# Pads that set where matmul operands lie, mod 512 bytes, in a two-block transformer kernel

## The chip, the core and the metric

The kernel runs on one core of a Trainium2 chip, as one program and one launch. The metric is the device time of a run in microseconds. The kernel before was timed in three runs: 1470.07, 1471.21 and 1471.54 us, median 1471.21 us.

## The reference

One sequence of 256 tokens with 1024 features goes through two layers of a first block and one layer of a second block, all in float32.

A layer of the first block computes

```
proj   = x @ w_in                       # queries, keys, values, gMLP halves, gates
out_a  = window_attention(...)          # 8 heads over 2 key heads, with a sink
out_b  = dense_block_attention(...)     # 8 heads over 2 key heads
out_c  = spatial_gating(u, v, ...)      # gMLP
merged = (branches @ w_branch * sigmoid(gate + b_gate)).sum over the branches
x = layer_norm(ALPHA * x + merged @ w_mix_out)
x = layer_norm(ALPHA * x + cross_attention(x, mem) @ x_wo)
x = layer_norm(ALPHA * x + gated_conv_ffn(x) @ f_w_down)   # 1024 -> 2 x 2816 -> 1024
```

The second block normalises x, takes one large product with w_in, runs a gated linear recurrence over 1344 channels and a sparse attention of 16 heads, merges both through gates, and adds an MLP of width 4096:

```
merged = sigmoid(g_a) * (y_a @ proj_a) + sigmoid(g_b) * (y_b @ proj_b)
h = x + merged @ w_out
out = h + square(relu(rmsnorm(h) @ w_mlp_in)) @ w_mlp_out
```

Nearly all of the arithmetic is the weight products.

## The kernel before

**Weights.** Class `Stream` brings the weights from HBM in the order of their use, in chunks of 128 partitions by 1024 float32 (512 KB), into four rotating tiles `raw`. Each chunk is split: ScalarE writes a rounded float32r part `wh` (L220), VectorE the rest `wl` (L221). There are four tiles of each, and two chunks are split ahead of the one in use.

**Products.** Activations are kept in two float32r parts too, so a product is three matmuls: high by high, low by high, high by low. There are two forms.

- `mm_a` (L402 to L404) gives a feature-major result. A 128x128 piece of the weight chunk is the stationary operand, and 256 tokens of activations (128x256) are the moving one. A chunk holds eight pieces, so it gives 24 matmuls.
- `mm_b` (L416 to L418, and L427, L455 to L458 for first chunks) gives a token-major result. A 128x128 piece of activations is stationary, and 512 columns of the weight chunk (128x512) are moving.

Each matmul is preceded by its own load of the stationary operand, which TensorE's queue starts while the matmul before is still streaming.

**The activations' tiles.** `fm` (`fmh`, `fml`) holds the features of the running x, or a merged result, for `mm_a` (gates, u, up, min and so on) and for `mm_b` (qa, v, mix, wq ...). `o` (`oh`, `ol`) holds a branch's output, moving in the `br` products (L402 to L404) and stationary in `wo`. `mem` holds the memory; `a` (`ah`, `al`) the FFN's hidden layer, stationary in `down`; `ya` the recurrence's output, moving in `pa`; `mg` the second block's merged result, stationary in `wo2`; `z` (`zh`, `zl`) the last MLP's hidden layer, stationary in `mout`.

**Order.** TensorE's instructions stand in the order in which the program is written, with attention units put in between at fixed ticks (`tick`, L341); the other engines' are ordered by the scheduler, in favour of what was written first. Nothing in the change touches these. Around a sublayer's end (`finish`, L570) the last chunks of a product and the first of the next are placed in other free room (`w0` to `w3`, `k4`, `a` and `fm` tiles).

**Places.** Tiles are laid out in SBUF by stacked pools: `base`, `w` (`raw`, `wh`, `wl`), `fm`, `sm`, then pools that are opened and closed by sublayer. A tile's place is the sum of the sizes before it, and since most sizes are multiples of 512 bytes a partition, all weight tiles `wh` and `wl` of the stream lie at 128 mod 512, and so do all `fm` tiles.

Of the kernel before, what the change touches and what calls it, by code (L numbers as in the profile page):

```python
# [47 lines left out]
def pack_a(w, nw=128, kw=128, per=8):  # L48
    """[K, N] -> one chunk of `per` stationary tiles after the other, N outer and K inner."""
    k, n = w.shape  # L50
    t = w.reshape(k // kw, kw, n // nw, nw).transpose(2, 0, 1, 3).reshape(-1, kw, nw)
    c = t.shape[0] // per
    return np.ascontiguousarray(t.reshape(c, per, kw, nw).transpose(0, 2, 1, 3).reshape(c, kw, per * nw))


def pack_b(w):
    """[K, N] -> chunks of two 128-row tiles of 512 columns, N outer and K inner."""
    k, n = w.shape
    t = w.reshape(k // 128, 128, n // 512, 512).transpose(2, 0, 1, 3).reshape(-1, 2, 128, 512)
    return np.ascontiguousarray(t.transpose(0, 2, 1, 3).reshape(-1, 128, 1024))  # L60


def feat(v, w=128):
    """[..., N] -> [w, ..., N // w]: features on partitions."""
# [11 lines left out]
def layout(x):  # L76
    """The arrays the program reads: the inputs cut and ordered, and constants of the shapes."""
# [96 lines left out]
class Stream:  # L174
    """The weights in the order of their use: each chunk comes in ahead of its products and is split
    into two float32r parts whose sum is the float32 weight."""
# [10 lines left out]
    def load(self, i, piece=None):  # L187
# [7 lines left out]
        else:  # L195
            # the very first chunk, in two pieces of 512 columns
# [46 lines left out]
    def take_last(self, key, places, more):  # L243
        """The last chunks of a product, as many as places and two, and those behind them, all on chip at once;
        those behind the first two have their room in places, the third one behind and on in more."""
# [5 lines left out]
    def hold(self, after):  # L251
        """The next chunks are split after the instructions `after`."""
# [3 lines left out]
class Program:  # L256
    def __init__(self, ctx, tc, a, out):
# [41 lines left out]
        # products that raise the tensor engine's clock while the first loads are on their way  # L299
# [21 lines left out]
    # ---- small helpers  # L321
# [18 lines left out]
    # ---- the order of the tensor engine: a tick before the products of each chunk  # L340
    def tick(self):  # L341
        """Gives out what is due, then a step of everything in the background."""
# [14 lines left out]
    def spawn(self, g):  # L357
        """Runs the first step of g now, the others a tick apart."""
# [3 lines left out]
    def wait(self):  # L362
        """What follows on the vector engine comes after the split of the last chunk."""
        return self.tc.issue_after(self.w.last.ins)

    def settle(self):
        """Gives out all that is left in the background."""
# [3 lines left out]
    def rstd(self, pool, var, eps, n, scale=1.0):  # L371
        """(var * scale + eps) ** -0.5 in float32, Newton's method from the exponent halved."""
# [13 lines left out]
    def split(self, h, l, src):  # L386
        """float32r parts h + l of src (SBUF or PSUM)."""
# [7 lines left out]
    def mm_a(self, ps, w, xs, nw=128, kw=128, t0=0, start=True, stop=True):  # L395
        """ps [nw, S] += W^T x: stationary tiles t0.. of the chunk w against the feature-major xs."""
# [9 lines left out]
    def mm_b(self, outs, ws, xs, kt, ts=(0, 1)):  # L406
        """outs[t] [128, 512] += x W for chunk list ws covering k-tiles kt.. of kt_n."""
# [12 lines left out]
    def mm_b_first(self, outs, wt, xs):  # L420
        """mm_b with the very first chunk, in the order in which the parts come."""
# [8 lines left out]
    def proj_b(self, key, xs, kn=8):  # L430
        """Token-major product with a [K, 512] weight."""
# [9 lines left out]
    def proj_first(self, key, xs):  # L441
        """Token-major product with a [1024, 512] weight, one token tile after the other; yields, each time with
        the outputs, before the passes of a token tile with the low parts of xs[:4] and xs[4:], and at the end."""
# [17 lines left out]
    def proj_second(self, key, xs, n):  # L461
        """Token-major product with a [1024, 512] weight: its first n chunks with the first token tile, then,
        after a yield, the rest; yields the outputs at the end."""
# [9 lines left out]
    def turn(self, outs, n, done):  # L473
        """Feature-major tiles [128, 2, S] of a token-major product: done(i, tile) n ticks later."""
# [15 lines left out]
    def take_early(self, key):  # L490
        """Takes the chunks that come before the next one of `key`."""
# [3 lines left out]
    def proj_last(self, key, xs, kn, places, more, done):  # L495
        """Token-major product with a [K, 1024] weight, the first token tile done some chunks ahead of the
        second. done(t, half, out) follows as soon as an output is whole; yields after each token tile."""
# [23 lines left out]
    def q(self, op, *args, **kw):  # L521
        """An instruction of the vector engine in the order of these calls."""
# [3 lines left out]
    def norm_fm(self, t, sq, scale, eps, first, second):  # L526
        """Token tile t of a norm: second(first(), rstd) by halves; returns the halves. The square root runs
        beside `first`; one step of Newton's method makes 1 / sqrt a float32."""
# [15 lines left out]
    def to_fm(self, t, halves, dst):  # L544
        """Token tile t, by halves, to its feature-major high parts in dst, then the low parts."""
# [20 lines left out]
    def rooms(self, tiles):  # L566
        """Places of weight chunks in tiles of high and low parts, two each."""
        return [[t.rearrange("p k t -> p (k t)")[:, i * 1024:i * 1024 + 1024] for t in tiles] for i in range(2)]

    def finish(self, wkey, xs, kn, add, norm, key, lead=None, more=0, room=None, second=()):  # L570
        """The end of a sublayer: its last product and norm, a token tile after the other, then the norm's
        feature-major parts and their first product, with the weight `key`, which occupies the tensor engine
        while the second tile's norm is on its way; lead fills the wait for the first one. With `second`, two
        more places, the first chunks of `key` come early, and a second product with `key` follows."""
# [1066 lines left out]
```

## Time and profile before

| | |
|---|---|
| median of three timed runs | 1471.21 us |
| profiled execution, first to last instruction (its span; the page gives no other time of it) | 1467.7 us |
| TensorE busy | 1446.2 us, 99% of the span |
| VectorE, ScalarE, GpSimd busy | 1083.6, 889.3, 46.0 us |
| TensorE instructions | 9919 matmuls, 9919 loads of the stationary operand |
| moved from HBM | 254.89 MB, 174 GB/s over the span |

The timed runs are some 3.5 us longer than this span. Matmuls overlap in the pipeline: one lists 0.28 us (256 columns) or 0.40 us (512 columns) from start to end, but the next starts long before that end. What a matmul takes of the span is therefore the distance between two starts, called its cadence here; it is read from the start times in the timeline, or from a window's length and its count (a window counts every matmul that overlaps it, which is about two more than start in it).

### The profile page before, as it was taken

The numbers are of one execution on the slowest core, as the hardware profiler recorded it, in microseconds if no ns is written. First come the engines' busy times: TensorE is split into PE (matmuls) and PEld (weight loads), VectorE is DVE, ScalarE is ACT, GpSimd is POOL, SyncE is SP. The second block draws the span as 40 slices with busy tenths as digits, with TensorE's granted clock in tenths as the row PEclk, the third lists the DMA queues.
The fourth block names the chain that finished last, engine by engine and source line by source line (L and its number), as shares of the span: only waits on it lengthen the run. The fifth ranks groups of instructions, "written<-read, shape, count | busy, mean of one in ns | idle before, by whom it ended". The sixth has DMA issues, their size and how long they took to land.

```text
span 1467.7 us, 26006 instructions
## 1 busy us (share of the span) xinstructions
PE 1446.2 (99%) x9919; PEld 1315.4 (90%) x9919; DVE 1083.6 (74%) x2195; ACT 889.3 (61%) x1608; POOL 46.0 (3%) x134
## 2 busy tenths in 40 slices
PE   9999999999999999999999999999999999999998
PEld 7889988899988899998889998788989999899887
DVE  6887576788857888668688885886889785866543
ACT  5866555666645586555666665464888775555432
POOL 1110000000000020000000000120100000000000
PEclk9999999999999999999999999999999999999999
DMA  8554574555566544454736566356544445555563
GB/s 314 172 159 158 177 225 127 187 188 186 179 186 216 186 145 147 141 197 164 253 105 205 184 199 221 129 171 190 172 121 141 134 149 168 191 164 183 185 202 99
DMA packets 75192, 257.63 MB, mean 176 GB/s; under 512 B 9787, under 2 KB 11196, under 8 KB 74940
## 3 DMA queue, kind: packets, MB, share of 16 engines
q1 hardware_dynamic: 75067, 255.97, 54.5%
q8 instruction: 78, 1.28, 0.3%
q14 instruction: 47, 0.38, 0.1%
HBM read 254.89 MB, written 1.05 MB: 174 GB/s over the span
## 4 chain that ended last, share of the span: by engine, by line
PE 82%; DVE 7%; ACT 5%; DMA 3%; issue 2%; POOL 1%; SPq 0%; DVEq 0%; ACTq 0%; POOLq 0%
PE mm L402 15%; PE mm L403 15%; PE mm L404 15%; PE mm L417 8%; PE mm L418 8%; PE mm L416 8%; DVE wl L221 2%; PE mm L455 2%; PE mm L457 2%; PE mm L458 1%; ACT wh L220 1%; PE tp L718 1%; PE tp L757 1%; PE tp L552 1%; PE sc L680 1%
## 5 line engine op out<-in xcount | busy, mean ns | idle before, releaser
L221 DVE TENSOR_TENSOR wl<-raw,wh 128x1024 fp32r<-128x1024 f32 (+3 forms) x434 | 521.0, 1206 | 236.8 <-ACT wh L220 230.7
L220 ACT CAST wh<-raw 128x1024 fp32r<-128x1024 f32 (+3 forms) x434 | 447.1, 1036 | 403.9 <-PE mm L403 141.3
L402 PE MATMUL mm<-fmh,wh 128*128 128x256 f32 (+1 forms) x1736 | 493.8, 284 | 3.8 <-ACT gates L957 1.7
L403 PE MATMUL mm<-fml,wh 128*128 128x256 f32 (+1 forms) x1736 | 490.6, 283 | 0.0
L404 PE MATMUL mm<-fmh,wl 128*128 128x256 f32 (+1 forms) x1736 | 490.6, 283 | 0.0
L402 PEld LDWEIGHTS mm<-fmh,wh 128*128 128x128 f32 (+1 forms) x1736 | 329.1, 190 | 9.1 <-issue 2.9
L403 PEld LDWEIGHTS mm<-fml,wh 128*128 128x128 f32 (+1 forms) x1736 | 329.2, 190 | 0.2
L404 PEld LDWEIGHTS mm<-fmh,wl 128*128 128x128 f32 (+1 forms) x1736 | 329.4, 190 | 0.0
L416 PE MATMUL mm<-wh,fmh 128*128 128x512 f32 x204 | 81.1, 397 | 0.5 <-ACT wh L220 0.5
L417 PE MATMUL mm<-wl,fmh 128*128 128x512 f32 x204 | 79.8, 391 | 0.8 <-DVE wl L221 0.8
L418 PE MATMUL mm<-wh,fml 128*128 128x512 f32 x204 | 79.9, 392 | 0.0
L416 PE MATMUL mm<-wh,ah 128*128 128x512 f32 x168 | 66.4, 395 | 0.0
L417 PE MATMUL mm<-wl,ah 128*128 128x512 f32 x168 | 66.4, 395 | 0.0
L418 PE MATMUL mm<-wh,al 128*128 128x512 f32 x168 | 66.3, 395 | 0.0
L402 PE MATMUL mm<-oh,wh 128*128 128x256 f32 x192 | 54.4, 283 | 0.0
L404 PE MATMUL mm<-oh,wl 128*128 128x256 f32 x192 | 53.8, 280 | 0.0
L403 PE MATMUL mm<-ol,wh 128*128 128x256 f32 x192 | 53.8, 280 | 0.0
L417 PE MATMUL mm<-wl,zh 128*128 128x512 f32 x128 | 50.6, 395 | 0.0
L418 PE MATMUL mm<-wh,zl 128*128 128x512 f32 x128 | 50.6, 395 | 0.0
L416 PE MATMUL mm<-wh,zh 128*128 128x512 f32 x128 | 50.6, 395 | 0.0
L1057 ACT ACTIVATE k<-mm,featp 128x256 f32<-128x256 f32 x88 | 48.6, 559 | 0.0
L417 PEld LDWEIGHTS mm<-wl,fmh 128*128 128x128 f32 x204 | 38.4, 188 | 8.7 <-DVE wl L221 1.1
(391 smaller groups left out, 2635.4 us busy)
## 6 DMA issues: line engine op xcount, KB each, us to landing
raw<-in_up_dram SPq DMA_DIRECT2D x80, 512.0 KB, 3.5
raw<-in_gate_dram SPq DMA_DIRECT2D x48, 512.0 KB, 3.5
raw<-in_down_dram SPq DMA_DIRECT2D x44, 512.0 KB, 3.5
raw<-in_mout_dram SPq DMA_DIRECT2D x32, 512.0 KB, 4.3
raw<-in_min_dram SPq DMA_DIRECT2D x28, 512.0 KB, 3.6
raw<-in_br_dram SPq DMA_DIRECT2D x24, 512.0 KB, 3.5
raw<-in_mix_dram SPq DMA_DIRECT2D x16, 512.0 KB, 3.5
raw<-in_wo_dram SPq DMA_DIRECT2D x16, 512.0 KB, 3.5
```

The lines of the kernel that those rows point to most:

```text
L220: self.nc.scalar.copy(h[:p, :w], r[:p, :w])
L221: self.last = self.nc.vector.tensor_sub(l[:p, :w], r[:p, :w], h[:p, :w].bitcast(F32))
L402: self.nc.tensor.matmul(ps, wh[:kw, c], xh[k], start=start and k == 0, stop=False)
L403: self.nc.tensor.matmul(ps, wh[:kw, c], xl[k], start=False, stop=False)
L404: self.nc.tensor.matmul(ps, wl[:kw, c], xh[k], start=False, stop=stop and k == n - 1)
L416: self.nc.tensor.matmul(outs[t], xh[:, k, r], wh[:, c], start=k == 0, stop=False)
L417: self.nc.tensor.matmul(outs[t], xh[:, k, r], wl[:, c], start=False, stop=False)
L418: self.nc.tensor.matmul(outs[t], xl[:, k, r], wh[:, c], start=False, stop=k == k_all - 1)
L455: self.nc.tensor.matmul(outs[t], xl[:, k, r], wh, start=False, stop=k == 7)
L457: self.nc.tensor.matmul(outs[t], xh[:, k, r], wh, start=k == 0, stop=False)
L458: self.nc.tensor.matmul(outs[t], xh[:, k, r], wl, start=False, stop=False)
L1057: nc.scalar.activation(y[:, i], ps, AF.Identity, bias=cb[:, c:c + 1], scale=k[1])
```

## The change

A helper `pad` allocates a small tile in a pool and clears it on GpSimd, so that what is allocated behind it moves up. It is called with 192 bytes ahead of the `fm` pool, 480 ahead of `mem`, 320 at the head of the cross-attention and of the FFN pools (both layers), 32 twice in the second block, 352 in the MLP. In `mixer` two small tiles are allocated after `macc` and `o` instead of before. The rest of the diff takes out comments and docstrings, so line numbers shift by up to 11.

```diff
+    def pad(self, pool, size):
+        self.nc.gpsimd.memset(pool.tile([128, size // 4], F32, name="pad"), 0.0)
...
 def mixer
             row = a[f"row{l}"]
+            macc = pool.tile([128, 8, S], F32, name="macc")
+            o = {i: (pool.tile([128, 4, S], F32R, name="oh", bufs=2), pool.tile([128, 4, S], F32R, name="ol", bufs=2))
+                 for i in (2, 0, 1)}
             rowp = pool.tile([128, 264], F32, name="rowp")
             nc.sync.dma_start(rowp, row[None, :264].to_broadcast([128, 264]))
             hb = pool.tile([128, 24], F32, name="hb")
-            macc = pool.tile([128, 8, S], F32, name="macc")
-            o = {i: (pool.tile([128, 4, S], F32R, name="oh", bufs=2), pool.tile([128, 4, S], F32R, name="ol", bufs=2))
-                 for i in (2, 0, 1)}
...
 def cross
+            self.pad(pool, 320)
             qt = pool.tile([128, 4, S], F32, name="qt")
...
 def ffn
+            self.pad(pool, 320)
             ah = pool.tile([128, NFF, S], F32R, name="ah")
...
 def run
+        self.pad(ctx.enter_context(tc.tile_pool(name="gap", bufs=1)), 192)
         self.fmp = ctx.enter_context(tc.tile_pool(name="fm", bufs=1))
...
+        self.pad(fb, 480)
         self.mem = (fb.tile([128, 8, S], F32R, name="memh"), fb.tile([128, 8, S], F32R, name="meml"))
...
 def block2
+            self.pad(pool, 32)
             qt = [pool.tile([128, 8, S], F32R, name=f"qt{j}") for j in range(2)]
...
+            self.pad(pool, 32)
             cl = pool.tile([RW, RT], F32, name="cl")
...
+            self.pad(pool, 352)
             zh = pool.tile([128, 32, S], F32R, name="zh")
```

What this does to the places follows from the tile sizes alone. The distance in this table is the moving operand's byte address in its partition less that of the stationary operand, mod 512, the same for high and low parts and for all pieces of a product. The counts are matmuls in the program.

| moving | stationary | matmuls | distance before | distance after |
|---|---|---|---|---|
| fm, 256 columns | weights | 4632 | 0 | 192 |
| o | weights | 576 | 160 | 192 |
| ya | weights | 288 | 448 | 160 |
| mem | weights | 192 | 32 | 192 |
| weights, 512 columns | fm | 744 | 0 | 320 (24 of them other tiles to a: 192) |
| weights | a | 456 | 480 | 0 |
| weights | z | 384 | 32 | 0 |
| weights | o, mg | 96 | 480, 224 | 0 |
| weights | mem | 96 | 480 | 320 |
| weights in other room | fm | 96 | 160 | 128 |

So the words of the change hold for `a`, `z`, `o` and `mg`; as stationary operand `fm` goes from distance 0 to 320. Pieces that are 112 columns wide (`ur`, `ug` and the recurrence's gates, 792 matmuls) step through eight distances 64 apart, before and after, since a piece is 448 bytes long. Other matmuls keep their distances.

The order of the instructions is the same on TensorE, VectorE, ScalarE and the DMA queue. On GpSimd (POOL) nine clears are new. This is its queue at the start, before; `ident` is the identity matrix that the first products need:

```order
4 L1630 MEMSET const-uint8-127 128x1
5 L1637 UNCONDITIONAL_BRANCH
6 masks.py:197 MEMSET ident 128x128
7 masks.py:199 ISA
8 masks.py:199 AFFINE_SELECT ident<-ident 128x128
```

And now:

```order
4 L1641 MEMSET const-uint8-127 128x1
5 L1648 UNCONDITIONAL_BRANCH
6 masks.py:197 MEMSET ident 128x128
7 L324 MEMSET pad 128x48
8 L324 MEMSET pad 128x120
9 masks.py:199 ISA
10 masks.py:199 AFFINE_SELECT ident<-ident 128x128
```

Two clears have come between the two steps that make `ident`. The second place is GpSimd's queue where the second block begins, with the semaphores that each instruction waits for; `vcz`, `ks` and `pc` are tiles of the sparse attention. Before:

```order
80 L383 TENSOR_TENSOR rs_y_6257<-rs_y_6257,rs_t_6258 128x16 [waits Pool_49]
81 L1455 MEMSET vcz 128x512 [waits DMAHW3_49,DMAHW2_49,DMAHW4_49,DVE_49,PE_49]
82 L1457 MEMSET ks_10828 128x4 [waits DMAHW7_49,DMAHW5_49]
83 L1457 MEMSET ks_10829 128x4
84 L1460 MEMSET pc_10834 128x128
```

And now:

```order
84 L387 TENSOR_TENSOR rs_y_6268<-rs_y_6268,rs_t_6269 128x16 [waits Pool_49]
85 L324 MEMSET pad 128x80 [waits DMAHW7_49,DVE_49,PE_49]
86 L324 MEMSET pad 128x80 [waits DVE_49,PE_49,Pool_49]
87 L324 MEMSET pad 128x8 [waits DMAHW2_49,DMAHW3_49,DVE_49,DMAHW4_49,PE_49,Pool_49]
88 L1464 MEMSET vcz 128x512
89 L1466 MEMSET ks_10845 128x4
90 L1466 MEMSET ks_10846 128x4
91 L1469 MEMSET pc_10851 128x128
```

The clears of cross-attention and FFN (128x80) stand ahead in the queue, and the clear that takes the room of the second block (128x8) now waits for what `vcz` waited for. Elsewhere a few instructions of the other engines wait for one of the clears in addition: the first write of `ah` and its first matmul in each FFN, the second mixer's first steps, its `rowp` DMA and the second block's `fp` DMA.

## Rows read from the trace of the kernel before

**Rows 1.** The page: span, and busy time by engine
```profile
span 1467.7 us, 26006 instructions
PE 1446.2 (99%) x9919; PEld 1315.4 (90%) x9919; DVE 1083.6 (74%) x2195; ACT 889.3 (61%) x1608; POOL 46.0 (3%) x134
```

**Rows 2.** The page: the chain that ended last, by engine
```profile
PE 82%; DVE 7%; ACT 5%; DMA 3%; issue 2%; POOL 1%; SPq 0%; DVEq 0%; ACTq 0%; POOLq 0%
```

**Rows 3.** Groups by line and shape, TensorE: busy us, mean ns, idle before
```profile
L402 PE MATMUL mm<-fmh,wh 128*128 128x256 f32 x1544 | 439.0, 284 | 3.8 <-ACT gates L957 1.7 <-ACT macc L1559 1.4 <-ACT k L1064 0.4
L416 PE MATMUL mm<-wh,fmh 128*128 128x512 f32 x204 | 81.1, 397 | 0.5 <-ACT wh L220 0.5
L416 PE MATMUL mm<-wh,ah 128*128 128x512 f32 x168 | 66.4, 395 | 0.0
L402 PE MATMUL mm<-oh,wh 128*128 128x256 f32 x192 | 54.4, 283 | 0.0
L416 PE MATMUL mm<-wh,zh 128*128 128x512 f32 x128 | 50.6, 395 | 0.0
L402 PE MATMUL mm<-yah,wh 112*128 112x256 f32 x96 | 26.9, 280 | 0.0
L402 PE MATMUL mm<-memh,wh 128*128 128x256 f32 x64 | 18.4, 288 | 0.0
```

**Rows 4.** Windows: us, then busy us and (xcount) by engine, granted clock, DMA
```profile
310.00:390.00 80.00, 80.00 (x669) 80.00 (x669) 70.25 (x113) 51.42 (x85) 0.00 (x0) 1.00 0.62 197
412.00:462.00 50.00, 50.00 (x216) 40.27 (x215) 27.29 (x30) 22.79 (x27) 0.00 (x0) 1.00 0.62 202
1375.00:1455.00 80.00, 80.00 (x344) 64.26 (x344) 37.93 (x33) 30.72 (x31) 0.00 (x0) 1.00 0.56 177
```

**Rows 5.** Timeline, TensorE, products of q2 and k2: start us, us, instruction
```profile
948.71 0.39 PE L416 MATMUL sc<-wh,fmh 128*128 128x512 f32 x1
...
964.83 0.39 PE L418 MATMUL mm<-wh,fml 128*128 128x512 f32 x1
```

**Rows 6.** Timeline, TensorE, a branch product
```profile
115.61 0.28 PE L402 MATMUL mm<-oh,wh 128*128 128x256 f32 x1
...
118.31 0.28 PE L404 MATMUL mm<-oh,wl 128*128 128x256 f32 x1
```

**Rows 7.** Timeline, TensorE, the memory's keys
```profile
238.82 0.28 PE L404 MATMUL mm<-memh,wl 128*128 128x256 f32 x1
...
243.96 0.28 PE L403 MATMUL mm<-meml,wh 128*128 128x256 f32 x1
```

**Rows 8.** Timeline, TensorE, pa, one stretch
```profile
1160.93 0.28 PE L402 MATMUL mm<-yah,wh 112*128 112x256 f32 x1
...
1165.05 0.28 PE L404 MATMUL mm<-yah,wl 112*128 112x256 f32 x1
```

**Rows 9.** Timeline, TensorE, pa, another stretch
```profile
1153.74 0.28 PE L402 MATMUL mm<-yah,wh 112*128 112x256 f32 x1
...
1157.61 0.28 PE L403 MATMUL mm<-yal,wh 112*128 112x256 f32 x1
```

**Rows 10.** Timeline, TensorE, wo2
```profile
1257.15 0.40 PE L416 MATMUL mm<-wh,mgh 128*128 128x512 f32 x1
...
1265.31 0.40 PE L418 MATMUL mm<-wh,mgl 128*128 128x512 f32 x1
```

**Rows 11.** Groups by line and shape, POOL
```profile
L1455 POOL MEMSET vcz<- 128x512 f32 x1 | 0.5, 527 | 398.6 <-PE mm L455 398.6
L1460 POOL MEMSET pc<- 128x128 f32 x3 | 0.5, 204 | 0.0
```

**Rows 12.** Timeline, TensorE, the start
```profile
1.35 3.35 PE L302 MATMUL sc<-ident 128*128 128x128 f32 x14 [1.35 <-POOL ident masks.py:199]
5.41 1.22 PE L427 MATMUL mm<-wh,fmh 128*128 128x512 f32 x2 [0.70 <-ACT wh L204]
```

**Rows 13.** Window: the recurrence's stretch at a lower granted clock
```profile
1080.00:1090.00 10.00, 8.33 (x46) 7.79 (x47) 8.40 (x19) 8.32 (x25) 0.00 (x0) 0.66 0.58 184
```

## The prediction

> **What bounds the kernel now.** The page's first part comes first: TensorE is busy for 1446.2 of 1467.7 us, 99% [rows 1]. The chain of waits agrees: 82% of it is TensorE's own work, and no other engine has over 7% [rows 2]. So what counts is how soon one matmul's start follows another's, and where that is not what sets the end, 21.5 us of idle time at most stand against it.
>
> The groups by line list the matmuls' time as 280 to 284 ns for 256 columns and 395 to 397 for 512 [rows 3]. These overlap in the pipeline, so the reader should turn to windows and start times. In the FFN's `up` stage 669 matmuls overlap a window of 80 us [rows 4]; less the 2.3 that only hang over an edge (0.28 us long, 0.12 apart) that is 80/666.7 = 120.0 ns. This is the cadence of `fm` moving at distance 0. The same shape at other distances, by first and last start and the number of steps between:
>
> - 160 (`o`): 2.70 us in 23 steps, 117.4 ns [rows 6]
> - 32 (`mem`): 5.14 us in 44 steps, 116.8 ns [rows 7]
> - 448 (`ya`): 4.12 us in 35 steps, 117.7 ns [rows 8], and 3.87 us in 34 steps, 113.8 ns [rows 9]
>
> With 448 there are two cadences, which is worth a pause: same tiles, same distance, and a stretch keeps the one that it falls into when it begins. Of the nine unbroken stretches of `pa`, three run like rows 9 and six like rows 8; the mean is (3 x 113.8 + 6 x 117.7)/9 = 116.4 ns. At 0 nothing of the kind is seen: 120.0 is held for a whole stage.
>
> With the weights moving it is the other way round. Distance 0 is the fast one: 16.12 us in 71 steps, 227.0 ns [rows 5]. At 480 the window of `down` gives 50/(216 - 1.7) = 233.3 ns (0.40 us long, 0.23 apart, so 1.7 hang over) and at 32 that of `mout` 80/(344 - 1.7) = 233.7 [rows 4]; at 224 `wo2` has 8.16 us in 35 steps, 233.1 ns [rows 10]. So 6.4 ns more at any of these distances. 480 and 224 differ by 256 and agree; that is the ground, a thin one, on which I read 192 with the moving activations as I read 448.
>
> A rule of the Trainium skill speaks against all this: TensorE: Matmul & The Clock Gate, in "Step-by-step: what each phase is for", says that TensorE reads the moving and the stationary operand through two independent SBUF ports, and that loading the next weights takes nothing from the running matmul. By that rule places can't matter and the sum would be zero; the trace disagrees, with 120.0 against 113.8 ns for one shape [rows 4, 9].
>
> **The change part by part.** The counts by distance are those of the change's table; the groups [rows 3] hold them by line (1544 for one of three passes of `fm` moving, 4632 in all).
>
> A. `fm` moving, 0 to 192. No stretch of the trace has this distance. Bounds by the nearest rows: 113.8 if every stretch falls into the fast cadence, 117.7 if none does [rows 8, 9]; 120.0 is what it is now. I take the mean of `pa`, 116.4: 4632 x 3.6 = 16.7 us saved; by the bounds 10.7 and 28.7.
>
> B. `o` 160 to 192 (576 x 1.0 = 0.6 us saved), `mem` 32 to 192 (192 x 0.4 = 0.1 saved), `ya` 448 to 160 (288 x 1.0 = 0.3 lost): together 0.4 saved, with 116.4 and 117.4 for the two distances. By the bounds from 2.4 saved to 0.6 lost.
>
> C. `fm` stationary, 0 to 320 (24 matmuls of them 0 to 192): here the change works against itself, since one pad moves `fm` for both of its roles. 744 x 6.3 = 4.7 us lost, with 233.3, the value at every other distance seen. Below, nothing lost, if 320 should be like 0; I see no reason for that.
>
> D. `a`, `z`, `o` and `mg` stationary, 480, 32 and 224 to 0: 936 x (233.4 - 227.0) = 6.0 us saved. Nothing, if what is fast in rows 5 were those products and not their distance; 6.3 with `mout`'s 233.7 throughout. Distance 0 is seen over 71 steps there, so I take the 6.0. `mem` stationary (480 to 320) and the weights in other room (160 to 128) stay among the slow distances: 0.
>
> E. Nine clears on GpSimd: a clear of 128x128 takes 204 ns and those here are no larger than 128x120 [rows 11], so at most 1.8 us of an engine that is busy for 46 of 1467.7 [rows 1]. What could be late: the identity matrix, which now stands behind two clears, 0.4 us at most. The first products on it end at 4.70 us (1.35 + 3.35), and the first weight product starts at 5.41 after 0.70 us of waiting for ScalarE [rows 12]; that wait hides it, and without that cover it would cost 0.4. At the second block `vcz` waits 398.6 us for the last matmul that reads its room [rows 11]; the clear ahead of it inherits that wait, and what is queued behind it on GpSimd is `vcz` as before, 0.2 us later. The FFN's first write of `ah`, ScalarE's, waits for a clear that was free to run when the sublayer's room was, a whole product earlier. The `rowp` and `fp` DMAs, behind which the weights queue on SP, wait for clears of the sublayer that has ended, long done. I count 0; 1.8 if none of it were hidden.
>
> F. What comes back as waiting. Chunks arrive by the pace of TensorE in the big stages: in `up`, the densest, VectorE is busy for 70.25 of 80 us and ScalarE for 51.42 [rows 4], 88% and 64%, and TensorE can become 12% faster there before VectorE is the bound; 3 to 5% is asked. But at the sublayers' ends and in the recurrence TensorE waits for chains that it does not release itself. Of the 18% of the chain that is not TensorE's [rows 2] I let a tenth of the gain go: 1.5 us lost. Bounds 0 and 3.
>
> Sum: -16.7 - 0.4 + 4.7 - 6.0 + 0 + 1.5 = -16.9 us. Against the profiled execution that is a span of 1450.8 instead of 1467.7; the page gives no other time of it, and the median of the runs shown is 3.5 us above the span. I keep the 3.5: 1471.2 - 16.9 = 1454.3.
>
> **The rivals.**
>
> *All slow.* The long stretches of `up`, `min` and the gates all keep the cadence of rows 8. For it: six of nine do, and a stage of 960 matmuls is decided by a single entry. A then saves 10.7, and B loses 0.6: -10.7 + 0.6 + 4.7 - 6.0 + 1.5 = -9.9, 1461.3 us.
>
> *All fast.* They all fall into the cadence of rows 9: -28.7 - 2.4 + 4.7 - 6.0 + 3.0 = -29.4, 1441.8 us. For it three of nine; against it that six don't, though a single early disturbance may tip a stage either way, and the two layers' `up` stages are alike and will fall alike.
>
> *Places don't matter.* The cadences differ by what is computed, not by distance: then `fm` stays at 120.0 and nothing is gained, 1471.2 us. For it: each distance comes with its own tile in the trace, and `ya` has 112 rows where `fm` has 128. Against it: `o` and `mem` have 128 and are under 118 all the same, and `a`, `z` and `mg` agree at 233. This is also what the two-ports rule above would give.
>
> *Slower.* 192 is a bad distance for moving activations, as every distance but 0 is for moving weights. If leaving 0 costs them the same 6.3 ns, A turns from -16.7 to +29.2, and with B, C and D (-1.7) the run takes 1498.7 us. It decides once the cadence of `fm` at 192 is over 121.0 ns, where 4632 x 1.0 eats B to D and 2.9 us more. Against it: 32, 160 and 448 all lie below 120.
>
> The granted clock widens the range. Around 1085 us TensorE idles twice for over a microsecond, and a stretch follows with a granted clock of 0.66 over 10 us [rows 13], that is, part of it at 1.2 instead of 2.4 GHz, (1 - 0.66)/0.5 = 68% of the 10 us. Half speed for 6.8 us costs 3.4. A TensorE that waits more in the recurrence may bring another such stretch, or shift its waits and lose this one: 3.4 either way.
>
> **How the numbers follow.** A mix of both cadences 0.48, all slow 0.26, all fast 0.16, no effect 0.05, slower 0.05. The forecast is the mix, 1454 us; its own range, with A between 12 and 22 saved and a clock stretch either way, is 1447 to 1461. The range for 8 in 10 takes in all slow with 1.7 us to spare and all fast: 1441 to 1463. A change of under 0.2% (2.9 us) could not be told from none here. Faster is the first three, 0.90; no change 0.05; slower 0.05.
>
> **What would show it.** In the profile after, `up` in a window of 80 us should have some 689 matmuls instead of 669 (116.4 ns), between 682 and 705 for the two cadences; `down` and `mout` should have cadences of 227 instead of 233; the products of qa, v, mix, wq and q2 should have gone from 227 to 233; GpSimd should be busy for 1 to 2 us more, and VectorE's and ScalarE's busy times should be unchanged. I am wrong if `up` still runs at 120 or above, if the long stages run at 113.8 throughout, or if TensorE's idle time grows by more than 3 us.

## The result, and the profile after

Four runs of the changed kernel have a median of 1447.6 us (1441.45 to 1452.99); the kernel before has 1470.64 us beside it (1468.05 to 1471.54). The ratio is 0.9843, with an interval of 0.9814 to 0.9872: the change saves 23.0 us, where 17 were forecast. The profiled execution is the slowest of the four, 1452.99 us, so the rows below tell of 16.5 us of span, not of 23. Every run that lists both its time and its span has 1.8 us between them; by that the profiled execution of the kernel before was one of 1469.5 us, a little under its median.

The page's first part and its chain of waits, after [rows 1, 2]:

```profile
span 1451.2 us, 26030 instructions
PE 1425.2 (98%) x9919; PEld 1299.8 (90%) x9919; DVE 1082.8 (75%) x2195; ACT 890.3 (61%) x1608; POOL 47.4 (3%) x143
```

```profile
PE 83%; DVE 6%; ACT 6%; DMA 3%; issue 1%; POOL 0%; SPq 0%; DVEq 0%; ACTq 0%; POOLq 0%
```

TensorE lost 21.0 us of busy time and still makes the end. Its idle time has grown from 21.5 to 26.0 us. VectorE and ScalarE have what they had (0.8 less, 1.0 more), and GpSimd 1.4 us more, the nine clears.

The group of `fm` as the stationary operand, after [rows 3]: busy us, mean ns of one, idle time before:

```profile
L420 PE MATMUL mm<-wh,fmh 128*128 128x512 f32 x204 | 81.1, 398 | 1.6 <-ACT wh L220 1.6
```

Its busy time is what it was, but as before these durations overlap and say little. The cadence comes from windows. After [rows 4], for `up` of the first layer, `down`, `mout` (10 us earlier here), `up` of the second layer, and `min`; the columns are those of rows 4, and the count behind PE's busy time is the one to read:

```profile
310.00:390.00 80.00, 80.00 (x682) 80.00 (x681) 71.48 (x116) 51.67 (x86) 0.00 (x0) 1.00 0.61 198
412.00:462.00 50.00, 50.00 (x222) 41.43 (x221) 27.87 (x29) 23.56 (x25) 0.00 (x0) 1.00 0.64 209
1365.00:1445.00 80.00, 80.00 (x355) 66.27 (x354) 35.62 (x32) 28.48 (x27) 0.00 (x0) 1.00 0.51 167
772.00:842.00 70.00, 70.00 (x596) 70.00 (x596) 62.14 (x102) 45.10 (x76) 0.00 (x0) 1.00 0.59 196
1300.00:1340.00 40.00, 40.00 (x355) 40.00 (x354) 26.60 (x31) 23.26 (x30) 0.00 (x0) 1.00 0.57 192
```

Worked out as in the prediction (2.4 matmuls of 256 columns hang over a window's edge, 1.7 of 512): `up` 80/679.6 = 117.7 ns in the first layer and 70/593.6 = 117.9 in the second, down from 120.0; `min` 40/352.5 = 113.5; `down` 50/220.3 = 227.0 and `mout` 80/353.3 = 226.4, down from 233. So both cadences that were seen at 448 appear at 192, each held for a whole stage: the two `up` stages took the slow one, `min` the fast one.

The products of q2 and k2, whose stationary operand is `fm`, now at 320 [rows 5]; first and last of the same 72:

```profile
941.31 0.39 PE L420 MATMUL sc<-wh,fmh 128*128 128x512 f32 x1
...
957.55 0.39 PE L422 MATMUL mm<-wh,fml 128*128 128x512 f32 x1
```

16.24 us in 71 steps are 228.7 ns, against 227.0 before and the 233.3 that were forecast. Distance 320 is nearly as good as 0.

What came back in this execution shows in two places. First the waits of TensorE, by the timeline (in brackets the idle time before the instruction and what ended it). Before:

```profile
108.38 0.39 PE L402 MATMUL mm<-fmh,wh 128*128 128x256 f32 x1 [1.66 <-ACT gates L957]
...
723.51 0.63 PE L718 MATMUL tp<-ident,pr 128*128 128x128 f32 x4 [1.57 <-DVE pr L710]
...
932.18 1.09 PE L552 MATMUL tp<-ident,k 128*128 128x128 f32 x8 [1.52 <-DVE k L524]
```

And after:

```profile
107.94 0.39 PE L406 MATMUL mm<-fmh,wh 128*128 128x256 f32 x1 [2.40 <-ACT gates L961]
...
716.16 0.68 PE L722 MATMUL tp<-ident,pr 128*128 128x128 f32 x4 [2.00 <-DVE pr L714]
...
923.66 1.09 PE L556 MATMUL tp<-ident,k 128*128 128x128 f32 x8 [2.03 <-DVE k L528]
...
1076.92 0.37 PE L406 MATMUL mm<-xch,wh 112*112 112x256 f32 x1 [1.61 <-ACT lga L1298]
```

(`gates`, `pr`, `k` and `lga` are tiles that ScalarE or VectorE write and TensorE's next matmul reads.) In this trace TensorE waits 0.4 to 0.7 us longer at each; the wait for `lga` was 1.01 us before. That a faster TensorE comes to the same chains of VectorE and ScalarE earlier would explain it, but only the wait for `pr` bears it out in every trace: it is 1.84 to 2.11 us in the changed kernel and all experiments. The waits for `gates` and `k` differ as much between executions of one kernel (1.23 and 1.38 us in experiment 9).

The largest single growth is none of these. The row of L420 above has 1.6 us of waiting for `wh`, against 0.5 in rows 3; it is one wait, at 10.5 us. Before, the first products on the weights start 0.43 us apart until 10.3 us; in this trace they speed up at 6.7 us, are through earlier and wait for the next chunk instead. The change doesn't decide this: in experiments 4, 8 and 10, which pad `fm` too, these products are slow until 9.4 us or later, and that wait is at most 0.72 us.

Second, the granted clock behind these waits, by windows, after [rows 13]:

```profile
105.00:115.00 10.00, 7.61 (x52) 7.37 (x51) 8.94 (x15) 8.07 (x17) 0.00 (x0) 0.83 0.17 57
715.00:720.00 5.00, 3.84 (x20) 3.87 (x21) 2.95 (x7) 4.13 (x8) 0.00 (x0) 0.66 0.95 270
925.00:930.00 5.00, 5.00 (x15) 4.01 (x16) 4.82 (x13) 1.65 (x5) 0.00 (x0) 0.68 0.00 0
1075.00:1085.00 10.00, 8.39 (x59) 8.17 (x58) 6.49 (x15) 8.95 (x24) 0.00 (x0) 0.83 0.62 208
```

Behind each of the four waits of the timeline part of a stretch ran at 1.2 instead of 2.4 GHz: (1 - 0.83)/0.5 of 10 us is 3.4, then 3.4, 3.2 and 3.4, in all 13.4 us. Before there was one such place, 6.8 us [rows 13]. The 6.6 more cost half their length, 3.3 us. Experiments 9 and 11 show below that the length of a wait doesn't decide whether such a stretch follows.

### The profile page after: what moved, and what is told of

Its sections match the earlier page's. It is cut to its first block, busy times and chain, and to the rows that moved or that the text cites. A ratio compares the mean times of both kernels' runs of the same rounds, so it can differ in the third digit from the quotient of the medians.

```text
span 1451.2 us, 26030 instructions
## 1 busy us (share of the span) xinstructions
PE 1425.2 (98%) x9919; PEld 1299.8 (90%) x9919; DVE 1082.8 (75%) x2195; ACT 890.3 (61%) x1608; POOL 47.4 (3%) x143
## 4 chain that ended last, share of the span: by engine, by line
PE 83%; DVE 6%; ACT 6%; DMA 3%; issue 1%; POOL 0%; SPq 0%; DVEq 0%; ACTq 0%; POOLq 0%
PE mm L406 15%; PE mm L407 15%; PE mm L408 15%; PE mm L422 8%; PE mm L421 8%; PE mm L420 8%; DVE wl L221 2%; PE mm L461 2%; PE mm L459 2%; PE mm L462 2%; ACT wh L220 2%; PE tp L761 1%; PE tp L722 1%; PE tp L556 1%; PE sc L684 1%
## 5 line engine op out<-in xcount | busy, mean ns | idle before, releaser
L406 PE MATMUL mm<-fmh,wh 128*128 128x256 f32 (+1 forms) x1736 | 488.9, 282 | 5.1 <-ACT gates L961 2.4
L408 PE MATMUL mm<-fmh,wl 128*128 128x256 f32 (+1 forms) x1736 | 485.5, 280 | 0.0
L407 PE MATMUL mm<-fml,wh 128*128 128x256 f32 (+1 forms) x1736 | 485.4, 280 | 0.0
L406 PEld LDWEIGHTS mm<-fmh,wh 128*128 128x128 f32 (+1 forms) x1736 | 325.5, 187 | 10.6 <-issue 2.8
L407 PEld LDWEIGHTS mm<-fml,wh 128*128 128x128 f32 (+1 forms) x1736 | 324.4, 187 | 0.2
L420 PE MATMUL mm<-wh,fmh 128*128 128x512 f32 x204 | 81.1, 398 | 1.6 <-ACT wh L220 1.6
L420 PE MATMUL mm<-wh,ah 128*128 128x512 f32 x168 | 65.4, 389 | 0.0
L420 PE MATMUL mm<-wh,zh 128*128 128x512 f32 x128 | 49.8, 389 | 0.0
L420 PEld LDWEIGHTS mm<-wh,fmh 128*128 128x128 f32 x204 | 38.4, 188 | 9.6 <-ACT wh L220 2.0
```

Source lines behind the costliest of these rows:

```text
L406: self.nc.tensor.matmul(ps, wh[:kw, c], xh[k], start=start and k == 0, stop=False)
L407: self.nc.tensor.matmul(ps, wh[:kw, c], xl[k], start=False, stop=False)
L408: self.nc.tensor.matmul(ps, wl[:kw, c], xh[k], start=False, stop=stop and k == n - 1)
L420: self.nc.tensor.matmul(outs[t], xh[:, k, r], wh[:, c], start=k == 0, stop=False)
```

## The experiments

Each is the kernel before or the changed one with one edit, timed against the kernel before on the same chip. Where a mean cadence is given without a row, it is worked out from all start times of that kind in the trace, without those that a wait interrupted.

**1. Only the pad ahead of `fm`.** The kernel before with `fm` at 192 as moving and 320 as stationary operand; `a`, `z`, `o`, `mem` keep their distances (`ya` comes to 128, `mg` to 32).

```diff
+        self.pad(ctx.enter_context(tc.tile_pool(name="gap", bufs=1)), 192)
         self.fmp = ctx.enter_context(tc.tile_pool(name="fm", bufs=1))
...
+        self.pad(fb, 320)
...
+            self.pad(pool, 320)
             zh = pool.tile([128, 32, S], F32R, name="zh")
```

> The kernel before with the pad of 192 ahead of fm alone; what lies behind is moved on so that a, z, o and mem keep their old distances (ya gets 128 instead of 448, mg 32). Theory (the distance of moving from stationary operand sets the cadence): up runs at 113.4 or 117.8 ns instead of 120.0, fm as a stationary operand at about 229.5 instead of 227; down and mout stay at 233.3. The time is that of the changed kernel less what a, z, o and mg give there (some 7 us): 1449 to 1461, middle 1455. Rival (the gain is mostly that of the stationary tiles put at 0): 1464 to 1471, up near 120.

Measured: 1454.47 us (1454.19 to 1457.11), before 1470.9; ratio 0.9886 (0.9869 to 0.9903). Windows in `up` of the first and of the second layer:

```profile
320.00:390.00 70.00, 70.00 (x621) 70.00 (x620) 64.42 (x105) 48.53 (x78) 0.00 (x0) 1.00 0.67 203
772.00:842.00 70.00, 70.00 (x596) 70.00 (x596) 61.91 (x100) 45.65 (x75) 0.00 (x0) 1.00 0.64 196
```

70/618.5 = 113.2 ns in one layer, 117.9 in the other, for the same products at the same distance. The pad ahead of `fm` gives 16.4 us by itself, and which cadence a stage takes is not fixed by the distance. `fm` as the stationary operand runs at 229.8 ns, `a` and `z` stay at 233.3.

**2. All but that pad.** The changed kernel with `fm` at 0, the other pads resized so that the rest stays at its new distances.

```diff
-        self.pad(ctx.enter_context(tc.tile_pool(name="gap", bufs=1)), 192)
...
-        self.pad(fb, 480)
+        self.pad(fb, 160)
...
-            self.pad(pool, 32)
+            self.pad(pool, 224)
             qt = [pool.tile([128, 8, S], F32R, name=f"qt{j}") for j in range(2)]
...
-            self.pad(pool, 352)
+            self.pad(pool, 32)
             zh = pool.tile([128, 32, S], F32R, name="zh")
```

> The changed kernel without the pad ahead of fm, all else as in it: fm at distance 0 in both roles, o and mem at 192, a, z, o and mg at 0 as stationary operands. Theory: up at 120.0 ns again, 669 matmuls in 80 us; down and mout at 227; the time is the one before less 6 to 7 us: 1462 to 1466, and the runs lie as close together as those before (within 3 us), since 120.0 has no second cadence. Rival (the gain is mostly that of the stationary tiles): 1449 to 1455.

Measured: 1465.57 us (1463.16 to 1468.04); ratio 0.996 (0.9946 to 0.9974). Windows in `up` and `down`:

```profile
320.00:390.00 70.00, 70.00 (x585) 70.00 (x585) 61.02 (x100) 45.01 (x74) 0.00 (x0) 1.00 0.64 193
412.00:462.00 50.00, 50.00 (x223) 41.37 (x222) 27.78 (x32) 24.12 (x28) 0.00 (x0) 1.00 0.66 205
```

`up` stays at 120.1, `down` goes to 225.9 by the window and 226.9 by all its starts. 5.3 us saved; with the 16.4 of experiment 1 that makes 21.7 of the 23.0, so the two halves add up to within 1.3 us, though more of the stages ran fast in experiment 1 (mean of `fm` moving 114.9 ns, 116.0 in the changed kernel). The runs spread over 4.9 us, where under 3 was expected. One thing in this trace led to experiment 5: all eight stretches in which `o` at 192 follows `fm` at 0 without a wait fall into the fast cadence.

**3. The same distances at other places.** The changed kernel with 128 bytes more ahead of the weights.

```diff
+        self.pad(ctx.enter_context(tc.tile_pool(name="gapw", bufs=1)), 128)
```

> The changed kernel with 128 bytes more ahead of the weight tiles, so that weights and everything behind them lie 128 further and all distances among them are those of the changed kernel. Theory (only the distance counts): the same two cadences, 113.4 and 117.8 ns, in up and min, 227 in down and mout, 1441 to 1453 us. Rival (the place itself counts, as where other engines write at the same time): another cadence in up, 119 to 121 ns, and 1458 to 1470 us.

Measured: 1451.33 us (1445.6 to 1452.03); ratio 0.9853 (0.9832 to 0.9873). Windows in `up` and `min`:

```profile
320.00:390.00 70.00, 70.00 (x596) 70.00 (x595) 61.69 (x102) 45.73 (x76) 0.00 (x0) 1.00 0.63 192
1300.00:1340.00 40.00, 40.00 (x342) 40.00 (x341) 25.64 (x29) 22.23 (x29) 0.00 (x0) 1.00 0.59 185
```

Two of the cadences seen before and no new one: 117.9 in `up`, 40/339.6 = 117.8 in `min` (113.5 in the changed kernel); `a` and `z` have 226.9 and 226.7. For this one shift the distance counts, not the place.

**4. `fm` at 64** (64 moving, 448 stationary), the pads behind it resized; all else at the changed kernel's distances.

```diff
-        self.pad(ctx.enter_context(tc.tile_pool(name="gap", bufs=1)), 192)
+        self.pad(ctx.enter_context(tc.tile_pool(name="gap", bufs=1)), 64)
```

> The changed kernel with fm at 64 from the weights as moving operand (448 as stationary one), all else at its distances. Theory (the end of the stationary piece against the moving one's start counts, mod 256): the 112-column pieces at distances 0 and 256 before, whose ends lie as those of a 128-column piece at 64, settled at 113 to 114 ns within two matmuls; so at 64 the fast cadence is the only one, up and min at 113.4 throughout: 1433 to 1441 us, runs within 4 us. Rival (64 is one more distance with a cadence of 116 to 118): up at 116.5 to 118, 1446 to 1455 us.

Measured: 1458.45 us (1458.31 to 1462.02); ratio 0.9917 (0.9902 to 0.9932). The 72 products of q2 and k2, first and last:

```profile
942.13 0.39 PE L420 MATMUL sc<-wh,fmh 128*128 128x512 f32 x1
...
958.69 0.39 PE L422 MATMUL mm<-wh,fml 128*128 128x512 f32 x1
```

16.56/71 = 233.2 ns: at 448 the weights moving over a stationary `fm` do pay what the prediction charged for 320. `fm` moving has 117.7 ns at 64, and the fast cadence is not seen; a distance that lies 128 lower is not as good as 192. The theory of the expectation falls with that, and the time lies above the rival's range too: the stationary `fm` alone costs 3.8 us more here (744 x 5.1 ns).

**5 and 6. Does the entry decide the cadence?** The changed kernel with eight matmuls that nobody reads, once in each of the three long stages, behind 72 unbroken products. In 5 their moving operand lies at distance 0, in 6, the control, at 192.

```diff
+    def turnover(self, wt, xs):
+        d = self.sc()
+        for _ in range(8):
+            self.nc.tensor.matmul(d[:, 0], wt[0][:, :128], wt[0][:, 256:512], start=True, stop=True)
...
+                    if j == 5 and not i:
+                        self.turnover(wt, xs)
                     self.mm_a(ps, wt, self.fmk(xs))
```

In 6 the moving operand is `xs[0][:, 0]` instead.

> The changed kernel with eight more matmuls, once in each up stage (before the weights of the fourth pair of channel tiles) and once in min, whose moving operand is a piece of the weight chunk itself, at distance 0 from the stationary piece; nothing reads what they give. Theory (at 192 there are two steady cadences, and how a stretch is entered decides; in the run with fm at 0 all eight stretches that came to 192 straight from matmuls at 0 fell into the fast one): behind them up and min run at 113.3 ns in all three stages; eight matmuls cost 1 us each time; with up slow before, 816 x 4.4 ns = 3.6 us come back a stage: 1438 to 1446 us, the runs within 5 us. Rival (up is slow for what runs beside it there): 117.8 still, 1450 to 1455.

> The control to the one with eight matmuls at distance 0: the same eight matmuls at the same three places, their moving operand a piece of fm, at distance 192. Theory (distance 0 before them is what turns the cadence): behind the eight the cadence is in each stage the one ahead of them, and the time is that of the changed kernel plus 3 us, 1444 to 1456 us. Rival (any eight matmuls more would do): 113.3 behind them.

Measured: 1447.25 us (1445.52 to 1448.91), ratio 0.984 (0.9824 to 0.9855), with the eight at 0; 1450.67 us (1447.39 to 1453.88), 0.9863 (0.9845 to 0.9881), with those at 192. The two `up` windows, of 5:

```profile
320.00:390.00 70.00, 70.00 (x620) 70.00 (x619) 64.35 (x105) 48.14 (x79) 0.00 (x0) 1.00 0.64 202
772.00:842.00 70.00, 70.00 (x620) 70.00 (x619) 64.22 (x105) 48.49 (x78) 0.00 (x0) 1.00 0.63 202
```

And of 6:

```profile
320.00:390.00 70.00, 70.00 (x597) 70.00 (x596) 61.60 (x100) 45.73 (x75) 0.00 (x0) 1.00 0.60 192
772.00:842.00 70.00, 70.00 (x597) 70.00 (x596) 61.67 (x100) 45.06 (x75) 0.00 (x0) 1.00 0.60 194
```

620 against 597 in both layers, 113.3 against 117.7 ns: the stage had the slow cadence up to the eight matmuls at distance 0 and has the fast one for the 816 products behind them; eight at 192 change nothing. `min` runs fast ahead of them and behind them either way. The moving operand of 5 is also another tile (the weights themselves) than in 6; no run separates that from its distance, but in experiment 2 the operand ahead was `fm`. The times differ by 3.4 us in the medians, and the intervals of the ratios overlap; the two stages give 2 x 816 x 4.4 ns = 7.2 by the cadence, so the trace settles it and the time alone wouldn't.

**7 and 8. `fm` at 224 and at 96** (stationary 288 and 416), edited as in 4; in 7 `ya` comes to 192 as well.

> The changed kernel with fm at 224 from the weights (288 as stationary operand). Theory: a distance has its own set of steady cadences, between 113.3 and 120; of those seen at 32, 64, 128, 160 and 192 only 192 has the fast one, so 224 should lie at 115 to 118, up near 117: 1448 to 1456 us. Rival (the fast cadence has a broad place around 192, and 224 keeps to it): 113.3, 1433 to 1441 us.

> The changed kernel with fm at 96 from the weights (416 as stationary operand). Theory: 64 gave 117.7 and ya at 128 gave 118.9, so 96 gives 117 to 119, and 416 costs as much as 448 did (233.3): 1456 to 1462 us. Rival (the cadence at 96 is a fast one of its own): under 116, 1440 to 1450 us.

Measured: 1459.31 us (1457.9 to 1462.22), ratio 0.9924 (0.9909 to 0.9938), at 224; 1466.13 us (1464.89 to 1470.29), 0.9973 (0.9963 to 0.9984), at 96. `up` of the first layer, at 224:

```profile
320.00:390.00 70.00, 70.00 (x594) 70.00 (x593) 61.98 (x102) 45.02 (x76) 0.00 (x0) 1.00 0.61 196
```

And at 96:

```profile
320.00:390.00 70.00, 70.00 (x585) 70.00 (x584) 60.99 (x101) 44.91 (x75) 0.00 (x0) 1.00 0.62 194
```

70/591.6 = 118.3 ns and 70/582.6 = 120.2: at 96 moving activations are no better off than at 0. Neither shows the fast cadence for `fm`, and both times lie above what was expected. With the weights moving, 288 gives 233.3 and 416 gives 234.0 ns. Put into the prediction's sum with the measured sizes of B and D (1.1 and 6.0, below), these cadences give, without a term for waiting, for 64, 224 and 96: 10.4 - 3.8 + 7.1 = 13.7, 7.4 - 3.8 + 7.1 = 10.7 and 0 - 4.3 + 7.1 = 2.8 us saved; measured are 12.4, 11.5 and 4.7.

**9 to 11. The changed kernel again, and a cheaper turn.** 9 is the changed kernel, unedited. 10 and 11 have two and one such matmuls at distance 0, in the `up` stages alone (`range(2)`, `range(1)` in the diff above, nothing in `min`).

> The changed kernel itself, beside the two that follow on the same chip. Its four times so far go from 1441.45 to 1452.99 us around 1447.6. If the cadence of a long stretch hangs on how it was entered, both up stages run at 117.8 ns again (some 724 matmuls in the 85 us from 315 to 400 us, as in its first trace) and the median comes within 1444 to 1451.

> The changed kernel with two unread matmuls whose moving operand lies at distance 0, once in each of the two up stages (none in the min stage, which runs at 113.3 ns without). Theory: two are enough to turn the entry. Then the 816 products behind them take 113.3 in place of 117.8 ns, 3.6 us in each stage, and the two cost 2 x 120 ns: 2 x (3.6 - 0.24) = 6.7 us under the changed kernel, some 752 matmuls from 315 to 400 us. Rival: it takes more than two, then 724 matmuls in that window and 0.5 us more than the changed kernel.

> The same with a single unread matmul in each up stage. If one product at distance 0 turns the entry: 2 x (3.6 - 0.12) = 7.0 us under the changed kernel and 752 matmuls from 315 to 400 us. If one is too few: 724 matmuls and within 0.5 us of the changed kernel. The second is a little likelier: the products settle over three to five matmuls when a stretch is entered.

Measured, before 1471.48: 1446.14 us (1445.19 to 1447.82), ratio 0.9832 (0.9818 to 0.9845), for 9; 1447.24 us (1446.68 to 1451.89), 0.9845 (0.9828 to 0.9862), for 10; 1442.63 us (1440.8 to 1446.4), 0.9814 (0.9797 to 0.9832), for 11. The two `up` windows of 9, then of 10, then of 11:

```profile
320.00:390.00 70.00, 70.00 (x597) 70.00 (x596) 61.92 (x102) 46.31 (x76) 0.00 (x0) 1.00 0.62 193
772.00:842.00 70.00, 70.00 (x597) 70.00 (x596) 61.76 (x101) 45.03 (x74) 0.00 (x0) 1.00 0.60 191
```

```profile
320.00:390.00 70.00, 70.00 (x596) 70.00 (x596) 61.74 (x101) 45.70 (x75) 0.00 (x0) 1.00 0.60 193
772.00:842.00 70.00, 70.00 (x620) 70.00 (x619) 64.20 (x104) 48.03 (x78) 0.00 (x0) 1.00 0.64 199
```

```profile
320.00:390.00 70.00, 70.00 (x620) 70.00 (x619) 64.47 (x106) 48.36 (x79) 0.00 (x0) 1.00 0.65 202
772.00:842.00 70.00, 70.00 (x621) 70.00 (x620) 64.12 (x104) 48.32 (x79) 0.00 (x0) 1.00 0.65 197
```

A single matmul was enough to turn the first layer of 11, against the expectation. The timeline around it, with the unread one in the middle:

```profile
306.31 0.28 PE L411 MATMUL mm<-fmh,wh 128*128 128x256 f32 x1
...
310.43 0.28 PE L413 MATMUL mm<-fmh,wl 128*128 128x256 f32 x1
310.55 0.28 PE L329 MATMUL sc<-wh 128*128 128x256 f32 x1
...
311.38 0.28 PE L411 MATMUL mm<-fmh,wh 128*128 128x256 f32 x1
...
314.32 0.28 PE L413 MATMUL mm<-fmh,wl 128*128 128x256 f32 x1
```

4.12 us in 35 steps ahead of it, 117.7 ns; 2.94 us in 26 steps behind it, 113.1. The second layer of 11 needed no turn. Ahead of its single matmul, at 759.12 us:

```profile
755.04 0.28 PE L411 MATMUL mm<-fmh,wh 128*128 128x256 f32 x1
...
759.00 0.28 PE L413 MATMUL mm<-fmh,wl 128*128 128x256 f32 x1
```

3.96/35 = 113.1 ns: it was fast already, and stayed fast. And two don't do it reliably: in the first layer of 10 the stage ran fast up to them and slow behind them, in the second the other way round. The first layer of 10:

```profile
306.37 0.28 PE L413 MATMUL mm<-fmh,wl 128*128 128x256 f32 x1
...
308.41 0.28 PE L413 MATMUL mm<-fmh,wl 128*128 128x256 f32 x1
308.52 0.39 PE L329 MATMUL sc<-wh 128*128 128x256 f32 x2
308.76 0.28 PE L411 MATMUL mm<-fmh,wh 128*128 128x256 f32 x1
...
314.41 0.28 PE L411 MATMUL mm<-fmh,wh 128*128 128x256 f32 x1
```

2.04/18 = 113.3 ns ahead, 5.65/48 = 117.7 behind. So an interruption at distance 0 can change the cadence either way. In the three slow `up` stages that met one or eight of them the fast cadence followed; two turned one slow stage fast and one fast stage slow. A single one at 192 was not tried. Without an interruption the cadence was never seen to change within a long stage. The program of 10 is the changed kernel's up to its first insertion, and still that stage began fast, where both traces of the changed kernel (the first and 9) have it slow throughout: one program falls into either cadence from one execution to the next. What in the entry decides stays open.

11 has the lowest median of all, 3.5 us under the changed kernel beside it, but its interval overlaps that of 9, so it isn't shown to be faster, and part of its gain is the second layer, which was fast before the insertion. Of the 7.0 us that its cadences give, some came back: TensorE idles for 25.3 us there (span 1440.8, busy 1415.5) against 24.1 in 9 (1446.0, 1421.9).

9 serves for one more comparison, with the first trace of the same kernel. The wait for `gates` in 9, the window behind it, and two windows in which the clock fell:

```profile
108.90 0.39 PE L406 MATMUL mm<-fmh,wh 128*128 128x256 f32 x1 [1.23 <-ACT gates L961]
```

```profile
105.00:115.00 10.00, 8.77 (x75) 7.88 (x74) 7.97 (x14) 8.35 (x17) 0.00 (x0) 1.00 0.28 97
...
920.00:925.00 5.00, 4.76 (x17) 3.70 (x16) 4.75 (x15) 1.38 (x4) 0.00 (x0) 0.66 0.01 2
10.00:20.00 10.00, 8.11 (x27) 6.29 (x28) 7.89 (x13) 6.71 (x8) 0.00 (x0) 0.83 0.94 354
```

Here that wait was 1.23 us, not 2.40, and the clock behind it stayed at 2.4 GHz; but at 919.56 us a wait of 1.38 us for `k` was followed by a stretch at half speed. In 11 the wait for `gates` was longer than in any other trace, and the clock didn't fall:

```profile
108.82 0.38 PE L411 MATMUL mm<-fmh,wh 128*128 128x256 f32 x1 [2.52 <-ACT gates L966]
```

```profile
105.00:115.00 10.00, 7.48 (x66) 7.04 (x63) 8.05 (x14) 8.35 (x17) 0.00 (x0) 1.00 0.16 56
```

So the length of a wait alone doesn't tell whether half speed follows. In the execution of 9 half speed makes 6.8 us, as long as before, and idle time 2.6 more than before; its span is 1446.0, 5.2 under the first trace, with the same cadences in `up` and `min`.

## Why the prediction was right, and where it wasn't

The forecast was 1454.3 us, its span 1450.8. The profiled span is 1451.2, and the median of all runs, 1447.6, lies well inside the range. The mechanism held: places decide the cadence, 192 has the two cadences of 448, and the long stages divide between them. But the sum came out so close to the profiled span because two errors, C and F, cancel in that execution; against the median, 23.0 us saved, the forecast was 6.1 short, and most of that is C. By all start times of the two traces, uninterrupted cadences times counts:

| step | forecast us | measured us |
|---|---|---|
| A. `fm` moving, 0 to 192 | -16.7 | -17.6 (mean 119.9 to 116.0 ns) |
| B. `o`, `mem`, `ya` | -0.4 | -1.1 |
| C. `fm` stationary, 0 to 320 | +4.7 | +0.9 (228.2 to 229.5) |
| D. `a`, `z`, `o`, `mg` to 0 | -6.0 | -6.0 |
| E. clears on GpSimd | 0 | 0 |
| F. waiting that comes back | +1.5 | +7.3 (what is left) |
| span | -16.9 | -16.5 |

- **A** held, with its mean of both cadences: 116.4 forecast, 116.0 measured. That "the two layers' `up` stages are alike and will fall alike" held in this trace and isn't a law: in experiments 1 and 10 they fell differently. That 192 may be read as 448, on the thin ground of 224 and 480, held too.
- **B** gained more because `o` stretches at 192 are fast in part (117.8 to 115.7 ns).
- **C is a mis-sized term.** The price for "every other distance seen" is right for 288, 416 and 448 (233.3 to 234.0) and wrong for 320, the one that mattered, which costs 1.3 ns and not 6.3. It was taken from other distances, and no row had 320: "I see no reason" to treat it like 0 was no evidence, and the bound of nothing lost was the nearer one.
- **D** held to the tenth: distance 0 made `a` and `z` fast, not the products of rows 5 as such, and experiment 2 gives it without A and C.
- **E** held: of TensorE's waits only the one for `ident` ends with GpSimd, and it went from 1.4 to 1.5 us.
- **F is the other mis-sized term, in this execution.** The prediction named 3 us of idle growth as a sign that it is wrong, and idle time grew by 4.5. Of the places, "the sublayers' ends" and "the recurrence" were right for `k` and `lga`; the waits for `gates` and `pr` lie inside a mixer and a cross-attention, and 1.0 us came at the start and isn't the change's. With three more of the waits came a stretch at half speed, 3.3 us together (4.5 + 3.3 = 7.8, against 7.3 left). The clock was put into the range "either way" and not into the sum. In experiment 9, the same kernel with the same cadences, the span is 21.7 us under that of before, which leaves 2.1 for F, and by the medians 0.8 are left: so 1.5 isn't refuted as a mean, and F swings by 5 us between executions. The forecast fits an execution with bad luck in the clock; the median of the runs is lower.
- **The 3.5 us** between span and median were kept as if they belonged to the program. The runs have 1.8; by that the other 1.7 belong to the one execution that was profiled.
- **The rivals.** *All slow* came true in `up`, while `min` and the later stretches of the gates ran fast. *Places don't matter* falls: in experiments 1, 4, 7 and 8 the products of `up` differ by the room of `fm` alone, and run at 113.2 or 117.9, 117.7, 118.3 and 120.2 ns. This was also what the prediction took from the Trainium skill (TensorE: Matmul & The Clock Gate, "Step-by-step: what each phase is for", two independent read ports): for this stream of loads and matmuls the measurement disagrees with it. The prediction's own ground, 120.0 against 113.8 ns "for one shape", was weaker than it says, since `ya` has 112 rows and `fm` 128; these experiments keep the shape. *Slower* falls with A: the two cadences at 192 lie below 120.

The four runs spread over 11.5 us, those before over 3.5. A turn of both `up` stages is worth 7.2 us, of `min` 2.9 (648 x 4.4 ns), and a stretch of half speed of 3.4 us costs 1.7. That these make the spread is argued from the traces and not shown: the runs that weren't profiled can't tell, experiment 9 has the same kernel within 2.6 us, and experiment 8, without the two cadences of `fm`, spreads over 5.4.

## What to carry to other kernels

Where TensorE bounds a kernel and its matmuls stand densely, read the cadence of one shape for each distance between the two operands' addresses mod 512 bytes, and choose places by that table; an operand that is used in both roles has to be priced in both. When several distances are unseen, don't charge one value for all, but measure or bound each. Where one distance has two cadences, allow for either. And give the waits, with what the granted clock does behind them, a term of the sum with a range from several executions: one trace of this kernel had 7.3 us of it, another 2.1.

## What the runs showed of the hardware

- The cadence of a dense stream depends on the distance mod 512 of the two operands and, for the one shift of 128 bytes that was tried, not on their place (experiment 3); the pieces of one product, multiples of 512 bytes apart, share a cadence. Activations moving over 128x128 weights, 256 columns, in ns: 0: 120.0; 32: 116.8 [rows 7]; 64: 117.7; 96: 119.9; 128: 118.9 (`ya` in experiment 1); 160: 117.8; 192: 113.3 or 117.8; 224: 118.3; 448: 113.8 or 117.7 [rows 8, 9]. The values at 128 and 448 are those of `ya`, with 112 rows. Weights moving, 512 columns: 0: 226.7; 320: 229.5; 288, 448 and the rows before at 32, 224 and 480: 233 to 234; 416: 234.0.
- At 192 two cadences are stable, 113.3 and 117.8 ns, each for up to 888 products on end. A single matmul at another distance turned one into the other (experiment 11, first layer); eight at the same distance didn't (experiment 6).
- The granted clock behind a wait isn't told by the wait's length: at the same wait for `gates`, 1.66 us before, 1.23 in experiment 9 and 2.52 in experiment 11 left it at 2.4 GHz, and 2.40 us in the changed kernel was followed by 3.4 us at 1.2 GHz, as was a wait of 1.38 us for `k` in experiment 9.
